# Stick-breaking attention summed by parts, with the value chain two tiles behind, 13 weight tiles and a woven last chunk

## The chip, the cores and the metric

The kernel runs on one NeuronCore of a Trainium2 chip. The metric is device time in microseconds (us) of one execution. TensorE (PE) does matrix products and transposes, VectorE (DVE), ScalarE (ACT) and GpSimd (POOL) do the elementwise work, SyncE (SP) issues nearly all DMAs, in order.

## What is computed

One decoder layer, 2048 tokens of 1024 numbers: a modulated RMS norm, one projection whose columns feed three token mixers (gated MLP, mLSTM, stick-breaking attention with 6 heads of 64), gates, an output projection and a residual. The change is in the attention:

```python
log_not = jnp.where(strict, jax.nn.log_sigmoid(-z), 0.0)
suffix = lax.cumsum(log_not, axis=3, reverse=True) - log_not
a = jnp.where(strict, jnp.exp(jax.nn.log_sigmoid(z) + suffix), 0.0)
outs.append(jnp.einsum('bhts,bshd->bthd', a.astype(vb.dtype), vb))
```

With b = sigmoid(z) and S[s] the product of (1 - b) over the keys from s on, a weight is a[s] = b[s] S[s+1], which is S[s+1] - S[s].

## The kernel before

Tokens are handled in 16 tiles of 128, in three blocks of 5, 5 and 6 tiles (`BLOCKS`). A block projects its tokens chunk by chunk of 384 columns (8 K-steps, three passes each because operands are split into a high and a low part, 24 matmuls for a token tile), and does the attention in three pairs of heads. For each pair `c_proj` makes q, k and v (evacuated by `c_evac` into Qst, Kst and Vst), then `stick` runs over units: one query tile i, one head h, up to four key tiles. A unit goes through `front` (two matmuls z, two sigmoids bb and be on ACT, masks on POOL, a running product backwards over bb on DVE, and the product be times bb, on DVE and POOL in turn), one step later `middle` (PE transposes, ACT copies the high part, DVE subtracts for the low part aT), another step later `back` (matmuls av with Vst), and `fin` (fold, copy yc, store). `interleave` mixes the units with the block's other projections, the fillers `bqk_proj`, `bg_proj`, `cz_proj`, `a_proj`; the value chunk of the mLSTM, `bv_proj` (tiles pv), follows the third pair. In the third pair of the first two blocks `get_x` also prepares the next block's x tiles, with a scaling on DVE and an addition on POOL (line 149). After the last block, pools are released and an output stage runs (out_proj, `mlstm`).

The order on each engine is set by a list scheduler that works with estimated times and priorities (`STK` puts stick ahead, `HIGH` the weight loads), so that instructions written later can stand earlier. Each engine then runs its own list strictly in order. The pools set further limits: `wr` holds 11 weight tiles, `bb` 4 and `be` 3 tiles of a unit.

Of the kernel before, what the change touches and what calls it, by code (L numbers as in the profile page):

```python
# [8 lines left out]
F32 = mybir.dt.float32  # L9
# [3 lines left out]
ALU = mybir.AluOpType  # L13
# [4 lines left out]
P = 128  # L18
# [14 lines left out]
def hybrid_block_kernel(ctx: ExitStack, tc: tile.TileContext, x, c, norm_g, w_ada, b_ada, w_in,  # L33
# [54 lines left out]

    lw = ExitStack()
    stg_p = lw.enter_context(tc.tile_pool(name="stg", bufs=2))  # L90
    wr_p = lw.enter_context(tc.tile_pool(name="wr", bufs=11))


    rs = ExitStack()
# [114 lines left out]
    brow = [stk.tile([P, 512], F32, tag="bb", bufs=4, name=f"brow{n}") for n in range(4)]  # L209
    for n in (2, 0, 3, 1):  # L210
        nc.gpsimd.memset(brow[n], 0.0)
    g_bc = [stk.tile([P, 512], F32, tag="be", bufs=3, name=f"g_bc{n}") for n in range(2)]

    def ada_load(half):
        for n, c0 in enumerate((1024 + 512 * half, 512 * half)):
# [86 lines left out]
    def c_proj(b, t0, nb, p):  # L302
# [17 lines left out]
            prev = nxt  # L320
        run(prev)

    def c_evac(b, t0, p, j, ps):
# [9 lines left out]
        nc.gpsimd.tensor_tensor(rr, rr, neghalf[:, 0:4], ALU.pow)  # L333
        nc.scalar.copy(Vst[:, i, :, 0:64], ps[:, 256:384].rearrange("p (h d) -> p h d", h=2))
        nc.vector.tensor_tensor(Vst[:, i, :, 64:128], ps[:, 256:384].rearrange("p (h d) -> p h d", h=2),
                                Vst[:, i, :, 0:64].bitcast(F32), ALU.subtract)
        qk = tmp.tile([P, 4, 2, 64], F32, tag="t512", bufs=T5, name=f"qk{p}_{i}")
        nc.vector.tensor_tensor(qk, ps[:, 0:256].rearrange("p (a d) -> p a d", a=4).unsqueeze(2)
                                .to_broadcast([P, 4, 2, 64]),
                                rr.unsqueeze(2).unsqueeze(3).to_broadcast([P, 4, 2, 64]), ALU.mult)  # L340
        yield
        pt = pat.tile([P, 4, P], F32, tag="at", name=f"pq{p}_{i}")
        for a in range(4):
            nc.tensor.transpose(pt[:, a, :], qk[:, a].rearrange("p r d -> p (r d)"), ident)
        ks = Kst[:, :, i * P:(i + 1) * P]
        gq, gk = prm[:, R_GQ:R_GQ + 1], prm[:, R_GK:R_GK + 1]
        nc.scalar.activation(ks, pt[:, 2:4, :], AF.Copy, scale=gk)
        nc.scalar.activation(Qst[:, j, 0], pt[:, 0:2, :], AF.Copy, scale=gq)
        nc.vector.scalar_tensor_tensor(ks[64:128], pt[64:128, 2:4, :], gk[64:128], ks[64:128].bitcast(F32),
                                       ALU.mult, ALU.subtract)  # L350
        nc.vector.scalar_tensor_tensor(Qst[:, j, 1], pt[:, 0:2, :], gq, Qst[:, j, 0].bitcast(F32),  # L351
                                       ALU.mult, ALU.subtract)
        if b < len(BLOCKS) - 1:
            nc.sync.dma_start(k_d[p][:, :, i * P:(i + 1) * P], ks.bitcast(F32))
            nc.sync.dma_start(v_d[p][:, i], Vst[:, i].bitcast(F32))

    def stick(p, t0, nb):
        units = []
# [450 lines left out]
    for b, nb in enumerate(BLOCKS):  # L809
# [22 lines left out]
        tail = bv_proj(t0, nb)  # L832
        if last:
            run(tail)
        else:
# [208 lines left out]
```

## Time and profile before

| | us |
|---|---|
| median of three runs (1478.18 to 1483.52) | 1481.43 |
| the profiled execution | 1480.27 |
| its span, first to last instruction | 1478.5 |
| PE busy | 1400.6 (95%) |
| DVE busy | 1025.1 (69%) |
| ACT busy | 678.1 (46%) |
| POOL busy | 647.3 (44%) |
| mean granted PE clock | 0.982 of full |

Busy time of PE is modelled at its ends and overlaps, so what counts for the end is where PE stands still (or runs at the lower clock), and which engine it waits for there. The stages of the span: setup until 76.6; the pairs of the first block from 76.6, 172.9 and 282.2; the second block's from about 377, 498.4 and 616.6; the last block's from 737, 909.7 and 1083.3; the output stage from 1215.6.

### The profile page before, as it was taken

The numbers are of one execution on the slowest core, as the hardware profiler recorded it, in microseconds if no ns is written. First come the engines' busy times: TensorE is split into PE (matmuls) and PEld (weight loads), VectorE is DVE, ScalarE is ACT, GpSimd is POOL, SyncE is SP. The second block draws the span as 40 slices with busy tenths as digits, with TensorE's granted clock in tenths as the row PEclk, the third lists the DMA queues.
The fourth block names the chain that finished last, engine by engine and source line by source line (L and its number), as shares of the span: only waits on it lengthen the run. The fifth ranks groups of instructions, "written<-read, shape, count | busy, mean of one in ns | idle before, by whom it ended". The sixth has DMA issues, their size and how long they took to land.

```text
span 1478.5 us, 24942 instructions
## 1 busy us (share of the span) xinstructions
PE 1400.6 (95%) x8468; PEld 1302.7 (88%) x8468; DVE 1025.1 (69%) x1778; ACT 678.1 (46%) x1656; POOL 647.3 (44%) x1140
## 2 busy tenths in 40 slices
PE   4999999889999999999999899999999978999998
PEld 3789999879999999988899799989999867888887
DVE  6796555586894566588698975778778888444443
ACT  3365444444464355446367655555455655211210
POOL 4463554573443433455233353433344336534442
PEclk9999999999999999999999999999999998999999
DMA  9866766657635534625332343303432524555551
GB/s 319 305 203 216 249 213 190 207 187 240 203 114 194 175 114 137 213 98 184 114 117 78 104 148 131 104 27 107 158 100 74 190 89 128 185 152 159 171 156 57
DMA packets 187103, 233.19 MB, mean 158 GB/s; under 512 B 22714, under 2 KB 160344, under 8 KB 186976
## 3 DMA queue, kind: packets, MB, share of 16 engines
q1 hardware_dynamic: 186752, 231.59, 48.1%
q8 instruction: 67, 1.10, 0.3%
q14 instruction: 60, 0.49, 0.1%
q0 software_dynamic: 224, 0.02, 0.0%
HBM read 159.24 MB, written 72.31 MB: 157 GB/s over the span
## 4 chain that ended last, share of the span: by engine, by line
PE 68%; DVE 16%; DMA 5%; issue 4%; POOL 3%; ACT 3%; SPq 1%; DVEq 0%; POOLq 0%; ACTq 0%
DVE bb L391 6%; PE av L421 5%; PE pc L296 4%; PE pc L298 4%; PE at L406 4%; PE pc L297 4%; PE po L957 4%; PE po L959 3%; PE po L958 3%; PE pg L298 3%; PE pg L297 3%; PE pg L296 3%; PE pb L465 2%; PE pb L464 2%; PE z L378 2%
## 5 line engine op out<-in xcount | busy, mean ns | idle before, releaser
L391 DVE TENSOR_TENSOR_SCAN bb<-bb,bb 128x513 f32<-128x513 f32 x144 | 194.1, 1348 | 24.9 <-ACT bb L383 23.8
L395 POOL TENSOR_TENSOR be<-be,bb 128x512 f32<-128x512 f32 (+3 forms) x120 | 133.0, 1108 | 148.3 <-DVE bb L391 69.2
L409 DVE TENSOR_TENSOR aT<-at,aT 128x512 fp32r<-128x512 f32 (+3 forms) x240 | 142.7, 597 | 31.5 <-ACT aT L408 30.5
L421 PE MATMUL av<-aT,Vst 128*128 128x256 f32 x816 | 146.4, 296 | 15.0 <-DVE aT L409 12.1
L408 ACT CAST aT<-at 128x512 fp32r<-128x512 f32 (+3 forms) x240 | 127.1, 530 | 70.3 <-PE at L406 67.4
L383 ACT ACTIVATE bb<-z 128x512 f32<-128x512 f32 (+3 forms) x240 | 130.3, 544 | 54.5 <-PE z L379 44.2
L421 PEld LDWEIGHTS av<-aT,Vst 128*128 128x128 f32 x816 | 120.5, 192 | 27.0 <-DVE aT L409 19.2
L296 PE MATMUL pc<-wr,hT 128*128 128x384 f32 (+1 forms) x384 | 136.8, 358 | 7.6 <-DVE hT L290 5.7
L406 PE MATMUL at<-ident,be 128*128 128x128 f32 x816 | 132.8, 277 | 9.6 <-DVE Qst L351 4.5
L298 PE MATMUL pc<-wr,hT 128*128 128x384 f32 (+1 forms) x384 | 135.5, 353 | 1.6 <-DVE hT L290 1.5
L297 PE MATMUL pc<-wr,hT 128*128 128x384 f32 (+1 forms) x384 | 134.0, 349 | 0.0
L384 ACT ACTIVATE be<-z 128x512 f32<-128x512 f32 (+3 forms) x240 | 132.1, 550 | 0.0
L406 PEld LDWEIGHTS at<-ident,be 128*128 128x128 f32 x816 | 99.2, 142 | 19.0 <-DVE aT L409 8.0
L957 PE MATMUL po<-wo,yT 128*128 128x512 f32 x256 | 105.0, 410 | 0.3 <-ACT yT L946 0.3
L958 PE MATMUL po<-wo,yT 128*128 128x512 f32 x256 | 102.3, 400 | 1.9 <-DVE wo L864 1.9
L391 DVE TENSOR_TENSOR_SCAN bb<-bb 128x129 f32<-128x129 f32 (+3 forms) x96 | 86.9, 905 | 23.5 <-POOL bb L386 16.3
L959 PE MATMUL po<-wo,yT 128*128 128x512 f32 x256 | 101.5, 400 | 0.0
L382 POOL MEMSET bb<- 128x1 f32 x240 | 24.2, 101 | 168.4 <-DVE bb L391 118.1
L378 PE MATMUL z<-Kst,Qst 128*128 128x512 f32 (+3 forms) x240 | 92.7, 387 | 1.7 <-ACT be L384 1.6
L466 PE MATMUL pb<-hT,wr 128*128 128x320 f32 (+1 forms) x288 | 91.9, 324 | 2.4 <-DVE wr L190 2.4
L464 PE MATMUL pb<-hT,wr 128*128 128x320 f32 (+1 forms) x288 | 93.1, 324 | 0.6 <-DMA wr<-w_d 0.6
L465 PE MATMUL pb<-hT,wr 128*128 128x320 f32 (+1 forms) x288 | 92.2, 322 | 0.0
(272 smaller groups left out, 3905.2 us busy)
## 6 DMA issues: line engine op xcount, KB each, us to landing
wr<-w_d SPq DMA_DIRECT2D x160, 384.0 KB, 5.6
w_d<-wr SPq DMA_DIRECT2D x80, 384.0 KB, 3.5
wad<-in_w_ada_dram SPq DMA_DIRECT2D x8, 1024.0 KB, 6.8
xo<-in_x_dram SPq DMA_DIRECT2D x16, 512.0 KB, 3.7
out_dram<-o SPq DMA_DIRECT2D x31, 256.0 KB, 2.9
xt<-in_x_dram SPq DMA_DIRECT2D x15, 512.0 KB, 3.5
st<-in_w_in_dram SPq DMA_DIRECT2D x60, 128.0 KB, 3.7
wr<-w_d SPq DMA_DIRECT2D x16, 392.0 KB, 6.0
```

The lines of the kernel that those rows point to most:

```text
L296: nc.tensor.matmul(ps, lhsT=hT[:, 0, k, cols], rhs=wt[k][:, 0, :W], start=k == 0, stop=False)
L297: nc.tensor.matmul(ps, lhsT=hT[:, 0, k, cols], rhs=wt[k][:, 1, :W], start=False, stop=False)
L298: nc.tensor.matmul(ps, lhsT=hT[:, 1, k, cols], rhs=wt[k][:, 0, :W], start=False, stop=k == KT - 1)
L384: nc.scalar.activation(be[:, :w], z[:, :w], AF.Sigmoid)
L391: nc.vector.tensor_tensor_scan(rev, rev, rev, carry.get((i, h), 1.0), ALU.mult, ALU.bypass)
L395: eng.tensor_tensor(be[:, :w], be[:, :w], bb[:, 1:w + 1], ALU.mult)
L406: nc.tensor.transpose(at[:, s, :], be[:, s * P:(s + 1) * P], ident)
L409: nc.vector.tensor_tensor(aT[:, :nb_, 1, :], at[:, :nb_, :], aT[:, :nb_, 0, :].bitcast(F32), ALU.subtract)
L421: nc.tensor.matmul(flat(av), lhsT=Vst[:, s0 + s, h, :], rhs=flat(aT[:, s]), start=(s0 + s == i), stop=(s0 + s == 0))
L957: nc.tensor.matmul(po, lhsT=yT[:, 0, k, :], rhs=wo[k][:, 0, cs], start=k == 0, stop=False)
L958: nc.tensor.matmul(po, lhsT=yT[:, 0, k, :], rhs=wo[k][:, 1, cs], start=False, stop=False)
L959: nc.tensor.matmul(po, lhsT=yT[:, 1, k, :], rhs=wo[k][:, 0, cs], start=False, stop=k == KT - 1)
```

## The change

The sum over keys is rearranged: with a[s] = S[s+1] - S[s], the sum of a[s] v[s] is the sum of S[s] (v[s-1] - v[s]) plus v of the query tile's last key. So a unit needs only the running product (bb): the second sigmoid, its mask, the column of ones and the product be times bb go, `middle` transposes bb, and bb gets 6 buffers. Vst now holds differences of values. They need each row's predecessor, one partition up: ACT copies v out of PSUM into vt, a DMA writes it one row lower into dv (127 rows), another fetches row 0, POOL subtracts vt, ACT copies the high part into Vst and POOL subtracts for the low part. That second half, `values`, is called two tiles later. The last value row goes to DRAM (vl_d), is read back to all partitions (vlast) and is added when yc is made, on DVE instead of ACT's copy. Weight tiles go from 11 to 13, the scratch of software DMAs is cut to 4096 bytes, and in the last block `bv_proj` becomes a filler of the third pair.

```diff
-    wr_p = lw.enter_context(tc.tile_pool(name="wr", bufs=11))
+    wr_p = lw.enter_context(tc.tile_pool(name="wr", bufs=13))
...
+    def values(pool_after, act_after):
+
+        b, p, i, dv, vt = late.pop(0)
+        with tc.issue_after(pool_after.ins):
+            nc.gpsimd.tensor_tensor(dv, dv, vt, ALU.subtract)
+        dv2 = dv.rearrange("p (h d) -> p h d", h=2)
+        with tc.issue_after(act_after.ins):
+            nc.scalar.copy(Vst[:, i, :, 0:64], dv2)
+        nc.gpsimd.tensor_tensor(Vst[:, i, :, 64:128], dv2, Vst[:, i, :, 0:64].bitcast(F32), ALU.subtract)
+        if b < len(BLOCKS) - 1:
+            nc.sync.dma_start(v_d[p][:, i], Vst[:, i].bitcast(F32))
+
     def c_evac(b, t0, p, j, ps):
...
-        nc.scalar.copy(Vst[:, i, :, 0:64], ps[:, 256:384].rearrange("p (h d) -> p h d", h=2))
-        nc.vector.tensor_tensor(Vst[:, i, :, 64:128], ps[:, 256:384].rearrange("p (h d) -> p h d", h=2),
-                                Vst[:, i, :, 0:64].bitcast(F32), ALU.subtract)
+        rr_pow = nc.gpsimd.tensor_tensor(rr, rr, neghalf[:, 0:4], ALU.pow)
...
+            nc.sync.dma_start(dv[0:1, :], v_before[p][P - 1:P, :])
...
+        v_copy = nc.scalar.copy(vt, ps[:, 256:384])
+        nc.sync.dma_start(dv[1:P, :], vt[0:P - 1, :])
+        nc.sync.dma_start(vl_d[p * NT + i:p * NT + i + 1, :], vt[P - 1:P, :])
+        v_before[p] = vt
+        late.append((b, p, i, dv, vt))
+        if j >= 2:
+            values(rr_pow, v_copy)
...
-            bb = stk.tile([P, 513], F32, tag="bb", bufs=4, name=f"bb{nm}")
-            be = stk.tile([P, 512], F32, tag="be", bufs=3, name=f"be{nm}")
-            nc.gpsimd.memset(bb[:, w:w + 1], 1.0)
-            nc.scalar.activation(bb[:, :w], z[:, :w], AF.Sigmoid, scale=-1.0)
-            nc.scalar.activation(be[:, :w], z[:, :w], AF.Sigmoid)
+            bb = stk.tile([P, 512], F32, tag="bb", bufs=BB, name=f"bb{nm}")
+            front_act[0] = nc.scalar.activation(bb[:, :w], z[:, :w], AF.Sigmoid, scale=-1.0)
...
-                nc.gpsimd.affine_select(out=be[:, w - P:w], in_=be[:, w - P:w], pattern=[[-1, P]],
-                                        compare_op=ALU.is_gt, fill=0.0, base=0, channel_multiplier=1)
...
+                    nc.sync.dma_start(vlast[i], vl_d[p * NT + i:p * NT + i + 1, :].broadcast_to([P, P]))
...
-            eng = nc.gpsimd if len(st_count) % 2 else nc.vector
-            st_count.append(0)
-            eng.tensor_tensor(be[:, :w], be[:, :w], bb[:, 1:w + 1], ALU.mult)
...
-            nc.scalar.copy(yc, py[:, 0:P])
+            nc.vector.tensor_tensor(yc, py[:, 0:P], vlast.pop(i), ALU.add)
...
+            if late and n >= 2:
+                values(front_pool[0], front_act[0])
...
+            fillers[2] = (chain(fillers[2][0], bv_proj(t0, nb)), 2)
```

What it moves: VectorE in the third pair of the last block, around the units of query tile 14. The names give the tile, query tile, head and first key tile. Before:

```order
L395 TENSOR_TENSOR be_14_1_4_14235<-be_14_1_4_14235,bb_14_1_4_14234 128x512
L391 SCALAR_TENSOR_TENSOR bb_14_1_0_14259<-bb_14_1_0_14259,bb_14_1_4_14234 128x513
L409 TENSOR_TENSOR aT_14_1_12_14220<-at_14_1_12_14216,aT_14_1_12_14220 128x3x128
L427 TENSOR_TENSOR avt_14_0_14229<-av_14_0_14122,avs_14_0_14227 128x128
L409 TENSOR_TENSOR aT_14_1_8_14249<-at_14_1_8_14244,aT_14_1_8_14249 128x4x128
L391 SCALAR_TENSOR_TENSOR bb_15_0_12_14287<-bb_15_0_12_14287 128x513
L395 TENSOR_TENSOR be_15_0_12_14288<-be_15_0_12_14288,bb_15_0_12_14287 128x512
```

The same place in the changed kernel:

```order
L418 SCALAR_TENSOR_TENSOR bb_14_1_0_13840<-bb_14_1_0_13840,bb_14_1_4_13816 128x512
L463 TENSOR_TENSOR yc_13_13724<-py_13_13721,vlast_13_13375 128x128
L433 TENSOR_TENSOR aT_14_0_4_13749<-at_14_0_4_13744,aT_14_0_4_13749 128x4x128
L418 SCALAR_TENSOR_TENSOR bb_15_0_12_13872<-bb_15_0_12_13872 128x512
L433 TENSOR_TENSOR aT_14_0_0_13776<-at_14_0_0_13771,aT_14_0_0_13776 128x4x128
L418 SCALAR_TENSOR_TENSOR bb_15_0_8_13901<-bb_15_0_8_13901,bb_15_0_12_13872 128x512
```

The products are gone, one addition for each query tile came, and running product and aT alternate, aT five units behind instead of three.

GpSimd at the passage from `c_proj` to `stick` in the same pair (rr: the norm of q and k of a token tile; bb of the tile 10: its masks). Before:

```order
L332 TENSOR_SCALAR rr_15_13199<-rr_15_13199 128x4
L333 TENSOR_TENSOR rr_15_13199<-rr_15_13199,neghalf 128x4
L386 AFFINE_SELECT bb_10_0_8_13228<-bb_10_0_8_13228 128x128
L388 AFFINE_SELECT be_10_0_8_13229<-be_10_0_8_13229 128x128
L395 TENSOR_TENSOR be_10_0_4_13265<-be_10_0_4_13265,bb_10_0_4_13264 128x512
```

Now:

```order
L351 TENSOR_TENSOR rr_15_12732<-rr_15_12732,neghalf 128x4
L333 TENSOR_TENSOR dv_13_12634<-dv_13_12634,vt_13_12636 128x128
L412 AFFINE_SELECT bb_10_0_8_12767<-bb_10_0_8_12767 128x128
L333 TENSOR_TENSOR dv_14_12685<-dv_14_12685,vt_14_12687 128x128
L337 TENSOR_TENSOR Vst<-dv_13_12634,Vst 128x2x64
L412 AFFINE_SELECT bb_10_1_8_12843<-bb_10_1_8_12843 128x128
```

The masks of the first units stand behind subtractions that wait for the shifted copies (dv).

TensorE where the last matmuls of `bv_proj` stand among the units of the third pair. Before:

```order
L297 MATMUL pv_14742<-wr_7_14595,hT 128x384
L298 MATMUL pv_14742<-wr_7_14595,hT 128x384
L421 MATMUL av_13_0_13885<-aT_13_0_12_13853,Vst 128x256 x2
L437 MATMUL py_12_13888<-fold,avt_12_1_13862 128x64
L378 MATMUL z_13_1_4_13995<-Kst,Qst 128x512
L379 MATMUL z_13_1_4_13995<-Kst,Qst 128x512
L406 MATMUL at_13_0_4_13907<-ident,be_13_0_4_13868 128x128 x4
```

Now:

```order
L300 MATMUL pv_14048<-wr_7_13530,hT 128x384
L583 MATMUL psp_10_0_13508<-va_10_12791,wsT 128x384
L301 MATMUL pv_14048<-wr_7_13530,hT 128x384
L407 MATMUL z_14_0_4_13697<-Kst,Qst 128x512
L408 MATMUL z_14_0_4_13697<-Kst,Qst 128x512
L445 MATMUL av_13_0_13459<-aT_13_0_4_13485,Vst 128x256
L583 MATMUL psp_10_1_13512<-va_10_12791,wsT 128x384
L445 MATMUL av_13_0_13459<-aT_13_0_4_13485,Vst 128x256 x3
L430 MATMUL at_13_0_0_13545<-ident,bb_13_0_0_13474 128x128 x4
```

The scheduler had already put pv among the units before; behind the last pv stood 18 z units and 22 units to transpose, and now 14 and 21.

## Rows read from the trace of the kernel before

**Rows 1.** Stages: window, length, busy of PE, PEld, DVE, ACT, POOL; clock; DMA

```profile
76.60:172.90 96.30, 93.04 (x599) 90.35 (x598) 68.78 (x130) 51.44 (x139) 50.85 (x96) 1.00 0.67 214
172.90:282.20 109.30, 104.79 (x614) 102.25 (x613) 61.41 (x125) 47.18 (x133) 51.54 (x90) 0.97 0.66 209
282.20:351.80 69.60, 63.94 (x387) 60.27 (x385) 50.80 (x96) 38.71 (x109) 46.12 (x81) 0.95 0.61 197
...
616.60:704.00 87.40, 80.97 (x507) 76.63 (x505) 74.34 (x116) 52.67 (x132) 53.02 (x93) 0.98 0.47 156
704.00:742.00 38.00, 35.11 (x208) 34.23 (x209) 23.55 (x47) 12.66 (x36) 9.65 (x17) 0.96 0.42 126
742.00:909.70 167.70, 161.88 (x1016) 153.12 (x1015) 137.46 (x226) 104.59 (x222) 66.88 (x136) 1.00 0.33 106
909.70:1083.30 173.60, 171.47 (x1085) 164.43 (x1084) 132.56 (x216) 90.06 (x214) 68.40 (x137) 1.00 0.34 112
...
1166.00:1215.60 49.60, 38.42 (x235) 30.79 (x234) 44.50 (x57) 31.26 (x67) 18.72 (x35) 0.93 0.49 179
1215.60:1251.00 35.40, 29.48 (x161) 25.69 (x159) 26.38 (x37) 17.79 (x42) 24.06 (x23) 0.81 0.46 130
```

**Rows 2.** What PE waited for: total us, times, longest

```profile
PE av L421 <- DVE aT L409: 12.1, 13, 3.0
...
PE at L406 <- DVE Qst L351: 4.5, 2, 3.2
...
PE pq L344 <- DVE qk L338: 3.8, 2, 3.4
...
PE pb L466 <- DVE wr L190: 2.4, 2, 1.3
```

**Rows 3.** Groups by line: count, busy us, mean ns, idle before

```profile
L395 POOL TENSOR_TENSOR be<-be,bb 128x512 f32<-128x512 f32 (+3 forms) x120 | 133.0, 1108 | 148.3 <-DVE bb L391 69.2 <-ACT be L384 21.1 <-PE at L406 17.0
...
L384 ACT ACTIVATE be<-z 128x512 f32<-128x512 f32 (+3 forms) x240 | 132.1, 550 | 0.0
...
L395 DVE TENSOR_TENSOR be<-be,bb 128x512 f32<-128x512 f32 (+3 forms) x120 | 77.4, 645 | 3.4 <-POOL be L388 0.4
...
L427 DVE TENSOR_TENSOR avt<-av,avs 128x128 f32<-128x128 f32 x96 | 26.8, 279 | 21.0 <-ACT avs L425 18.0 <-PE py L437 2.6
...
L544 POOL TENSOR_TENSOR gu<-tb 128x128 f32<-128x128 f32 x32 | 20.0, 626 | 29.5 <-DVE tb L543 28.6 <-PE at L406 0.8
```

**Rows 4.** Groups by line on DVE in 1166 to 1215.6 us

```profile
L391 DVE TENSOR_TENSOR_SCAN bb<-bb,bb 128x513 f32<-128x513 f32 x14 | 19.6, 1401 | 0.6 <-ACT bb L383 0.5
...
L395 DVE TENSOR_TENSOR be<-be,bb 128x512 f32<-128x512 f32 (+1 forms) x9 | 6.9, 763 | 0.2
```

**Rows 5.** Timeline of DVE and POOL, third pair: start, duration

```profile
1191.96 1.27 DVE L391 TENSOR_TENSOR_SCAN bb<-bb,bb 128x513 f32<-128x513 f32 x1
...
1193.73 1.84 DVE L391 TENSOR_TENSOR_SCAN bb<-bb,bb 128x513 f32<-128x513 f32 x1
...
1193.40 1.09 POOL L395 TENSOR_TENSOR be<-be,bb 128x512 f32<-128x512 f32 x1 [1.92 <-ACT bb L383]
```

**Rows 6.** Timeline of POOL and DVE at the second block's third pair

```profile
626.46 5.29 POOL L149 TENSOR_TENSOR xt<-xt,hshift 128x1024 f32<-128x1024 f32 x2
...
627.13 2.37 DVE L395 TENSOR_TENSOR be<-be,bb 128x256 f32<-128x256 f32 x1
629.42 3.40 DVE L391 TENSOR_TENSOR_SCAN bb<-bb,bb 128x513 f32<-128x513 f32 x1
```

**Rows 7.** Timeline of PE inside a projection: start, duration

```profile
257.92 0.34 PE L296 MATMUL pc<-wr,hT 128*128 128x384 f32 x1
258.09 0.34 PE L297 MATMUL pc<-wr,hT 128*128 128x384 f32 x1
```

**Rows 8.** Landing of the 64 KB stores of yc (line 440)

```profile
DMA to landing us min/median/max: 1.5/3.4/7.5
```

**Rows 9.** The page's DMA queue: packets, MB, share of 16 engines

```profile
q1 hardware_dynamic: 186752, 231.59, 48.1%
```

More of the change, by code (lines that the diff above doesn't have):

```diff
@@ L27 @@
 T5 = 6
+BB = 6
 OFF = dict(au=0, av=256, az=512, bq=768, bk=1152, bv=1536, bo=1920, bz=2304, bi=2688,
@@ L53, in hybrid_block_kernel @@
     v_d = [dram.tile([P, NT, 2, P], F32, name=f"v_d{p}") for p in range(3)]
+    vl_d = dram.tile([3 * NT, P], F32, name="vl_d")
     ident = const.tile([P, P], F32, name="ident")
@@ L75, in hybrid_block_kernel @@
     gates = const.tile([P, 2, NT, 4], F32, name="gates")
+    vt_end = const.tile([P, 3, P], F32, name="vt_end")
     gT = const.tile([P, 64], F32, name="gT")
@@ L208, in hybrid_block_kernel @@
     crow = tmp.tile([8, P], F32, tag="t512", bufs=T5, name="crow")
-    brow = [stk.tile([P, 512], F32, tag="bb", bufs=4, name=f"brow{n}") for n in range(4)]
+    brow = [stk.tile([P, 512], F32, tag="bb", bufs=BB, name=f"brow{n}") for n in range(4)]
     for n in (2, 0, 3, 1):
         nc.gpsimd.memset(brow[n], 0.0)
-    g_bc = [stk.tile([P, 512], F32, tag="be", bufs=3, name=f"g_bc{n}") for n in range(2)]
+    g_bc = [stk.tile([P, 512], F32, tag="bb", bufs=BB, name=f"g_bc{n}") for n in range(2)]
     def ada_load(half):
@@ L321, in c_proj @@
         run(prev)
+    late = []
+    v_before = {}
+    def values(pool_after, act_after):
[8 more added lines that the diff above has]
+            nc.sync.dma_start(v_d[p][:, i], Vst[:, i].bitcast(F32))
     def c_evac(b, t0, p, j, ps):
@@ L332, in c_evac @@
         nc.gpsimd.tensor_scalar(rr, rr, 1.0 / 64, EPS, ALU.mult, ALU.add)
-        nc.gpsimd.tensor_tensor(rr, rr, neghalf[:, 0:4], ALU.pow)
-        nc.scalar.copy(Vst[:, i, :, 0:64], ps[:, 256:384].rearrange("p (h d) -> p h d", h=2))
-        nc.vector.tensor_tensor(Vst[:, i, :, 64:128], ps[:, 256:384].rearrange("p (h d) -> p h d", h=2),
-                                Vst[:, i, :, 0:64].bitcast(F32), ALU.subtract)
+        rr_pow = nc.gpsimd.tensor_tensor(rr, rr, neghalf[:, 0:4], ALU.pow)
+        dv = tmp.tile([P, P], F32, tag="dv", bufs=4, name=f"dv{p}_{i}")
+        if i == 0:
+            nc.gpsimd.memset(dv[0:1, :], 0.0)
+        else:
+            nc.sync.dma_start(dv[0:1, :], v_before[p][P - 1:P, :])
+        vt = vt_end[:, p, :] if j == BLOCKS[b] - 1 else tmp.tile([P, P], F32, tag="vt", bufs=4, name=f"vt{p}_{i}")
+        v_copy = nc.scalar.copy(vt, ps[:, 256:384])
[5 more added lines that the diff above has]
+            values(rr_pow, v_copy)
         qk = tmp.tile([P, 4, 2, 64], F32, tag="t512", bufs=T5, name=f"qk{p}_{i}")
@@ L354, in c_evac @@
             nc.sync.dma_start(k_d[p][:, :, i * P:(i + 1) * P], ks.bitcast(F32))
-            nc.sync.dma_start(v_d[p][:, i], Vst[:, i].bitcast(F32))
     def stick(p, t0, nb):
@@ L369, in stick @@
         st = {}
-        st_count = []
+        vlast = {}
+        front_act, front_pool = [None], [None]
         def front(u):
@@ L379, in front @@
             nc.tensor.matmul(z[:, :w], lhsT=Qst[:, j, 1, h, :], rhs=kk, start=False, stop=True)
-            bb = stk.tile([P, 513], F32, tag="bb", bufs=4, name=f"bb{nm}")
-            be = stk.tile([P, 512], F32, tag="be", bufs=3, name=f"be{nm}")
-            nc.gpsimd.memset(bb[:, w:w + 1], 1.0)
-            nc.scalar.activation(bb[:, :w], z[:, :w], AF.Sigmoid, scale=-1.0)
-            nc.scalar.activation(be[:, :w], z[:, :w], AF.Sigmoid)
+            bb = stk.tile([P, 512], F32, tag="bb", bufs=BB, name=f"bb{nm}")
+            front_act[0] = nc.scalar.activation(bb[:, :w], z[:, :w], AF.Sigmoid, scale=-1.0)
             if s1 == i + 1:
-                nc.gpsimd.affine_select(out=bb[:, w - P:w], in_=bb[:, w - P:w], pattern=[[-1, P]],
+                front_pool[0] = nc.gpsimd.affine_select(out=bb[:, w - P:w], in_=bb[:, w - P:w], pattern=[[-1, P]],
                                         compare_op=ALU.is_gt, fill=1.0, base=0, channel_multiplier=1)
-                nc.gpsimd.affine_select(out=be[:, w - P:w], in_=be[:, w - P:w], pattern=[[-1, P]],
-                                        compare_op=ALU.is_gt, fill=0.0, base=0, channel_multiplier=1)
-            rev = bb[:, 0:w + 1][:, ::-1]
+                if h == 0:
+                    vlast[i] = stk.tile([P, P], F32, tag="vlast", name=f"vlast{p}_{i}")
+                    nc.sync.dma_start(vlast[i], vl_d[p * NT + i:p * NT + i + 1, :].broadcast_to([P, P]))
+            rev = bb[:, 0:w][:, ::-1]
             nc.vector.tensor_tensor_scan(rev, rev, rev, carry.get((i, h), 1.0), ALU.mult, ALU.bypass)
             carry[i, h] = bb[:, 0:1]
-            eng = nc.gpsimd if len(st_count) % 2 else nc.vector
-            st_count.append(0)
-            eng.tensor_tensor(be[:, :w], be[:, :w], bb[:, 1:w + 1], ALU.mult)
-            st[u] = [be, None]
+            st[u] = [bb, None]
             return 2 * w / 2.4
@@ L401, in middle @@
             nm = f"{p}_{i}_{h}_{s0}"
-            be = st[u][0]
+            bb = st[u][0]
             nb_ = s1 - s0
@@ L405, in middle @@
             for s in range(nb_):
-                nc.tensor.transpose(at[:, s, :], be[:, s * P:(s + 1) * P], ident)
+                nc.tensor.transpose(at[:, s, :], bb[:, s * P:(s + 1) * P], ident)
             aT = stk.tile([P, 4, 2, P], F32R, tag="aT", bufs=3, name=f"aT{nm}")
@@ L831, in hybrid_block_kernel @@
             interleave(stick(p, t0, nb), stick_cost(t0, nb), fillers[p][0], fillers[p][1] * chunk)
[L832 to L835, printed above, removed]
+        if not last:
+            tail = bv_proj(t0, nb)
             t1, n1 = t0 + nb, BLOCKS[b + 1]
@@ L1029 @@
     from concourse.bass_utils import run_bass_kernel_spmd as _run
[L1031 removed]
+    nc = _bacc.Bacc("TRN2", target_bir_lowering=False, num_devices=1, dynamic_dma_scratch_size=4096)
     arrays, args = {}, []
```

1 line of the change is left out of this document (removed).

## The prediction

> **What bounds the kernel now.** I read the busy shares first, then the table of stages, then the list of what PE waited for, and last the timelines of the stages with the largest gaps. PE is busy 95% of the span and none of its matmuls is taken away, so the gain can be no more than the time in which PE stands or runs at the lower clock. In each stage I take the window's length less PE's busy time as idle, and the length times (1 - granted clock) as the most that the clock costs; the clock has two levels, 1.2 and 2.4 GHz, and falls here after PE has stood still. From [rows 1] (idle / clock, us): 3.3 / 0 at 76.6; 4.5 / 3.3 at 172.9; 5.7 / 3.5 at 282.2; 6.4 / 1.7 at 616.6; 2.9 / 1.5 at 704; 5.8 / 0 at 742; 2.1 / 0 at 909.7; 11.2 / 3.5 at 1166. That is 41.9 + 13.5 = 55.4 us in the attention stages. The output stage's first 35 us hold another 5.9 / 6.7, before which no attention work stands. The largest waits of PE are for DVE: av for aT 12.1 us, transposes held by Qst 4.5, pq by qk 3.8 [rows 2]. In 1166 to 1215.6 DVE is busy 44.5 of 49.6 us and PE 38.4 [rows 1]: there the units are paced by DVE, since no filler is left.
>
> **The change part by part.**
>
> *Removed.* POOL loses 120 products, 133.0 us, ACT 240 sigmoids, 132.1 us, DVE 120 products, 77.4 us [rows 3]; with them go the masks of be and the memsets on POOL. DVE's subtraction for Vst moves to POOL. Nearly all of this stood beside PE work, so the sums are not the gain: each stage has its own.
>
> *Tail of the third pair, 1166 to 1215.6.* Here DVE sets the pace. Nine products, 6.9 us, go [rows 4]. The running products average 1401 ns over 14 [rows 4], and one alone takes 1.27 us, one beside a POOL product 1.84 [rows 5]; with those POOL products gone, 14 x (1.401 - 1.27) = 1.8 us more. Three additions for yc come in, each taken as long as the avt addition, 279 ns [rows 3]: 0.8 us back. The woven chunk changes little: the scheduler had already put pv among the units, and behind its last matmul stand 14 z units instead of 18, 21 to transpose instead of 22. That brings some running products under cover; I take 1.6 us, a little over one of them. Sum 6.9 + 1.8 - 0.8 + 1.6 = 9.5 us, of at most 11.2 + 3.5. At 49.6 - 9.5 = 40.1 DVE still has 35 us of work against PE's 38.4, so PE comes next.
>
> The row first: beside a POOL product of 1.09 us a running product grew by 0.57 us, and 14 of them by 1.8 us together [rows 4, 5]. The Trainium skill (SBUF — State Buffer, section Who interferes with whom) says that a DVE instruction with two SBUF inputs and a GpSimd one that reads SBUF exclude each other for the whole instruction. By that rule each of the seven or so products on POOL would cost DVE up to 1.09 us, some 7.6 us in place of 1.8, and the forecast would be 6 us lower; the measured 1.8 decides.
>
> *742 to 909.7.* Idle 5.8 us with DVE busy 137.5 of 167.7 [rows 1]; the waits are those of av and transposes for aT [rows 2]. A product less in every second unit on DVE frees 645 ns each [rows 3]. I take 4 us, between 0 (the wait is latency, not load) and 5.8.
>
> *Third pairs of the first two blocks, 282.2 and 616.6.* The two additions of get_x occupy POOL for 5.29 us, and next to them a DVE product of 256 columns took 2.37 us and a running product 3.40 [rows 6]; behind both stands the evacuation of Qst for which PE waited 3.2 us [rows 2]. get_x stays, but the product of 2.37 us goes. I take 4.5 us of 6.4 + 1.7 at 616.6, and 4.5 of 5.7 + 3.5 at 282.2, where the same step stands; bounds 0 and all of it.
>
> *172.9 to 282.2.* PE waited 3.4 us for qk once [rows 2], and the clock fell. vt frees the PSUM tile sooner and two more weight tiles are fetched ahead, but whether the cause goes isn't seen: I take 2.5 of 7.8 us.
>
> *76.6 to 172.9.* The waits for weights being split, 2.4 us [rows 2], are what two more weight tiles and a freer POOL would shorten: 2 of 3.3 us. *704 and 909.7*: 1 and 1.5 us of 4.4 and 2.1.
>
> *The value chain* is what is added, for each of 48 token tiles: two POOL subtractions, 96 x 626 ns = 60 us [rows 3], less than half of what POOL loses; one more ACT copy, paid by the yc copy that ACT loses; and four DMAs (SP's list grows by 197 rows). I cost it at nothing because of its place: the shifted copy is issued when vt is there and wanted two tiles later, two times 24 matmuls at 0.17 to 0.18 us apart [rows 7], 8.4 us. A store of the same 64 KB lands after 3.4 us in the median and 7.5 at most [rows 8]. If that cover is gone, what waits is POOL's subtraction, and behind it in the same queue the norm of the next token tile (then qk, pq) and the masks of the first units (then the running product); ACT's copy into Vst also stands ahead of Kst and Qst evacuations. In the first two blocks the store of Vst follows it on SP, among weight loads. The price then is the first rival's.
>
> *The handover at 1215.6* keeps its steps: 0, between 12.6 us gained and 6 lost if the loads for the output stage, which wait for pv's weight buffers, come later than they did.
>
> **Sum.** 9.5 + 4 + 4.5 + 4.5 + 2.5 + 2 + 1 + 1.5 = 29.5 us. The profiled execution took 1480.3, 1.2 under the median of 1481.4; as a median the forecast is 1481.4 - 29.5 = 1452 us.
>
> **The rivals.**
>
> *The shifted value rows come too late (slower).* One partition up means 127 rows. Should this copy not be spread like the others but run on one DMA engine, the queue's rows give its time: 0.481 x 16 x 1478.5 us over 186752 packets is 61 ns each, over 231.59 MB it is 20 bytes in a ns [rows 9]; 127 packets of 512 bytes are 3.2 us by bytes, 7.7 by packets. With 1.5 us, the shortest landing [rows 8], that is 4.7 to 9.2 us against the 8.4 of cover, and the longest landings lie 4 us above the median. If every second of 48 tiles comes 1.5 us late, POOL and PE lose 36 us and the time is 1452 + 36 = 1488. From 0.6 us a tile on (29.5 / 48) it eats the whole gain. For it: the copy has no twin in the trace before. Against it: 3.2 us by bytes is nearer, since packets here average 1240 bytes. Chance 9%. The Trainium skill (DMA: Bandwidth & Descriptors, section Why a DMA increments its semaphore by 16 and not by 1) says that a transfer's engines must divide its slowest dimension, so that 127 partitions go to one engine; no row before can show that, and the rival's price does not need it.
>
> *Only the tail and the loaded stage gain.* The waits before 742 come with get_x's additions, with weight splitting and DMAs, which all stay; then 9.5 + 4 = 13.5 us, 1468. For it: POOL's additions alone slowed a running product to 3.40 us [rows 6]. Against it: the product between them goes. 20%.
>
> *Every wait of the attention stages goes*: 55.4 us, 1426. For it: ACT and POOL are each some 130 us lighter, and aT runs five units behind, not three. Against it: the tail can't lose its drain, and some waits have other causes. 13%.
>
> *PE bounds it all the same*: waits move to other places, first to the handover, which runs at a clock of 0.81 [rows 1], and the time stays at 1481. 8%.
>
> **How the numbers follow.** The forecast's case has 50%, its own range 1440 to 1464 from half and all of its uncertain terms. A measurement of this kernel can tell about 0.3%, 4.4 us, from no change. Faster: 50 + 20 + 13 = 83%; the same 8%; slower 9%. The range from 1432 to 1480 leaves out the late copies, half of the case in which every wait goes, and a little of the last.
>
> **What would show it.** Right: in the tail running products near 1.27 us and DVE no longer ahead of PE in busy time, the last pair some 9 us shorter, the third pairs of the first two blocks 4 to 5 each, no wait of POOL for the shifted copies. Wrong: pq or the first running product of a pair waiting for POOL behind dv; the copies of 127 rows landing past 8 us; the stretch from the last av to the first long run of output matmuls longer than before; or gaps of the get_x stages as they were.

## The result and the profile after

The changed kernel takes 1514.53 us (median, 1514.11 to 1520.51) against 1481.91 for the kernel before: ratio 1.0238, 95% interval 1.0216 to 1.0259. It is slower by 2.4%; the forecast was 1452, with a range to 1480. The profiled execution spans 1512.4 us, 33.9 more than before.

The page of the changed kernel: span, busy time, share and instructions of each engine, and its DMA queue, which answers to [rows 9].

```profile
span 1512.4 us, 24156 instructions
...
PE 1410.5 (93%) x8468; PEld 1312.5 (87%) x8468; DVE 939.8 (62%) x1658; ACT 577.5 (38%) x1416; POOL 503.5 (33%) x783
...
q1 hardware_dynamic: 201344, 237.91, 49.0%
```

DVE, ACT and POOL lost 85, 101 and 144 us of work, as the change intends, and PE waits longer all the same: of the 33.9 us, PE stands 24.0 longer and is busy 9.9 longer, at a mean granted clock of 0.974 for 0.982. Where, the windows tell (columns as in [rows 1], after's own stages).

```profile
82.50:183.50 101.00, 95.36 (x602) 90.91 (x602) 66.22 (x126) 49.26 (x130) 45.49 (x79) 1.00 0.70 226
183.50:294.20 110.70, 103.63 (x610) 101.19 (x609) 53.61 (x116) 42.36 (x120) 42.25 (x70) 0.97 0.67 208
294.20:363.80 69.60, 56.97 (x317) 54.15 (x316) 42.24 (x83) 28.04 (x84) 37.01 (x55) 0.88 0.56 180
...
398.40:532.60 134.20, 123.85 (x785) 118.57 (x784) 87.85 (x158) 53.63 (x130) 35.38 (x72) 0.96 0.50 163
...
1199.20:1248.80 49.60, 40.84 (x263) 34.33 (x262) 36.94 (x51) 22.05 (x46) 5.06 (x6) 0.97 0.61 202
```

Idle time (length less PE) is 12.6 us in the 69.6 from 294.2, where [rows 1] had 5.7, and the clock is 0.88 for 0.95. It is 10.4 us at 398.4, a stage that had next to none (PE 120.4 of 121.1 us before). The losses are in setup and the first two blocks. Setup and the first block load, split and store weights (the last weight store is issued at 337.1 us); the second block reads them back, as the third does. A row for each stage, from the first z of a pair to that of the next, in us, difference to before; the last three columns are runs told of below:

| stage of before | before | forecast | changed | no copies | split copy | by DRAM |
|---|---|---|---|---|---|---|
| 0 to 76.6 (setup) | 76.6 | 0 | +5.9 | +0.7 | +2.5 | +4.7 |
| 76.6 | 96.3 | -2 | +4.7 | -2.2 | +1.1 | +0.4 |
| 172.9 | 109.2 | -2.5 | +1.5 | -7.4 | -6.3 | -8.5 |
| 282.2 | 95.1 | -4.5 | +9.1 | +2.4 | +3.0 | +7.1 |
| 377.3 | 121.1 | 0 | +13.1 | +1.4 | +5.8 | +2.1 |
| 498.4 | 118.3 | 0 | +2.3 | -0.4 | -0.7 | -0.5 |
| 616.6 | 120.3 | -5.5 | +2.3 | -7.3 | -3.1 | -8.2 |
| 736.9 | 172.8 | -4 | -1.4 | -5.4 | -5.0 | -5.6 |
| 909.8 | 173.6 | -1.5 | -3.3 | -5.9 | -6.5 | -5.7 |
| 1083.3 (to the last py) | 131.8 | -9.5 | -0.5 | -3.9 | -4.0 | -2.6 |
| output | 263.4 | 0 | +0.2 | +0.6 | +0.3 | -0.1 |

What the engines waited for in the changed kernel (waiter and line, what ended it: total us, times, longest):

```profile
ACT wr L192 <- DMA st<-in_w_in_dram: 79.4, 27, 9.6
...
ACT Vst L336 <- POOL dv L333: 64.9, 25, 8.3
...
POOL dv L333 <- DMA dv<-vt_end: 35.9, 7, 7.9
...
PE z L407 <- ACT bb L410: 15.8, 10, 5.3
...
POOL dv L333 <- DMA dv<-vt: 13.1, 7, 5.9
```

Before, the first of these was:

```profile
ACT wr L189 <- DMA st<-in_w_in_dram: 50.9, 22, 7.2
```

and PE's z waited little for ScalarE:

```profile
PE z L378 <- ACT be L384: 1.6, 5, 0.6
```

GpSimd does wait for the shifted rows (49 us), as the first rival said, and 35.9 of it is for the last token tile of a block (vt_end). In the second and the last block the transfers of those copies make five of the fifteen longest pieces of the chain of work that ended last (start, length):

```profile
542.37 7.11 DMA dv<-vt_end
...
666.24 6.50 DMA dv<-vt_end
...
781.34 8.40 DMA dv<-vt_end
...
952.44 8.73 DMA dv<-vt_end
...
1123.18 7.82 DMA dv<-vt_end
```

But the largest new wait of PE, z held by bb, has another chain behind it, in the first block. SyncE's list at the second pair of the first block (start, time of the issue):

```profile
185.77 0.65 SPq L360 DMA_DIRECT2D dv<-vt  x1
186.48 1.00 SPq L361 DMA_DIRECT2D vl_d<-vt  x1
187.53 0.55 SPq L357 DMA_DIRECT2D dv<-vt  x1
188.17 1.23 SPq L196 DMA_DIRECT2D w_d<-wr  x2
189.45 0.76 SPq L171 DMA_DIRECT2D st<-in_w_in_dram  x1
...
193.72 0.68 SPq L360 DMA_DIRECT2D dv<-vt_end  x1
194.45 2.37 SPq L361 DMA_DIRECT2D vl_d<-vt_end  x1
```

and what waits, ScalarE's weight copy and then PE (in brackets idle time and what ended it):

```profile
194.12 0.93 ACT L192 CAST wr<-st 128x384 fp32r<-128x384 f32 x2 [9.57 <-DMA st<-in_w_in_dram]
...
196.31 0.69 PE L407 MATMUL z<-Kst,Qst 128*128 128x384 f32 x1 [4.41 <-ACT bb L410]
```

SyncE issues here without a pause, the weight piece (st) goes out at 189.45, ScalarE stands at its split until 194.12, and the Qst copy and the sigmoids behind it are late for PE. The row store (L361, one row of 512 bytes) mostly takes long to issue where it follows the shifted copy at once (columns: min/median/max ns, first and last start):

```profile
L361 SPq DMA_DIRECT2D vl_d<-vt x39: 294/999/4812, 62.1 to 1122.0; - x39
L361 SPq DMA_DIRECT2D vl_d<-vt_end x9: 1461/2370/4204, 88.3 to 1123.9; - x9
```

48 of them are 74.9 us of SyncE's time, for a DMA that moves 24 KB in all.

### The profile page after: what moved, and what is told of

Same layout as the page of the kernel before. It is cut to its first block, busy times and chain, and to the rows that moved or that the text cites. A ratio compares the mean times of both kernels' runs of the same rounds, so it can differ in the third digit from the quotient of the medians.

```text
span 1512.4 us, 24156 instructions
## 1 busy us (share of the span) xinstructions
PE 1410.5 (93%) x8468; PEld 1312.5 (87%) x8468; DVE 939.8 (62%) x1658; ACT 577.5 (38%) x1416; POOL 503.5 (33%) x783
## 4 chain that ended last, share of the span: by engine, by line
PE 62%; DMA 12%; DVE 11%; issue 4%; ACT 4%; POOL 3%; SPq 3%; DVEq 0%; POOLq 0%; ACTq 0%
PE av L445 5%; PE at L430 4%; PE po L982 4%; PE po L984 4%; PE po L983 4%; PE pc L299 4%; DVE bb L418 4%; PE pc L301 4%; PE pc L300 4%; DMA st<-in_w_in_dram 3%; DMA dv<-vt_end 3%; DMA wr<-w_d 2%; PE z L407 2%; PE z L408 2%; PE pg L301 2%
## 5 line engine op out<-in xcount | busy, mean ns | idle before, releaser
L418 DVE TENSOR_TENSOR_SCAN bb<-bb,bb 128x512 f32<-128x512 f32 x144 | 190.1, 1320 | 15.1 <-ACT bb L410 13.6
L445 PE MATMUL av<-aT,Vst 128*128 128x256 f32 x816 | 145.6, 293 | 17.9 <-DVE aT L433 11.2
L430 PE MATMUL at<-ident,bb 128*128 128x128 f32 x816 | 133.0, 278 | 7.2 <-DVE Qst L380 3.2
L430 PEld LDWEIGHTS at<-ident,bb 128*128 128x128 f32 x816 | 101.0, 143 | 15.1 <-DVE aT L433 4.8
L412 POOL TENSOR_SCALAR_AFFINE_SELECT bb<-bb 128x128 f32<-128x128 f32 x96 | 40.4, 422 | 180.5 <-ACT bb L410 148.4
L418 DVE TENSOR_TENSOR_SCAN bb<-bb 128x128 f32<-128x128 f32 (+3 forms) x96 | 83.3, 869 | 25.8 <-POOL bb L412 25.2
L490 PE MATMUL pb<-hT,wr 128*128 128x320 f32 (+1 forms) x288 | 95.4, 331 | 4.0 <-ACT wr L192 3.1
L299 PE MATMUL pa<-wr,hT 128*128 128x384 f32 x256 | 90.6, 354 | 6.7 <-DMA wr<-w_d 4.0
L491 PE MATMUL pb<-hT,wr 128*128 128x320 f32 (+1 forms) x288 | 94.2, 328 | 0.0
L492 PE MATMUL pb<-hT,wr 128*128 128x320 f32 (+1 forms) x288 | 93.7, 328 | 0.0
L299 PE MATMUL pg<-wr,hT 128*128 128x384 f32 x256 | 89.5, 350 | 1.8 <-DMA wr<-w_d 1.8
```

Of the source, the lines that this page charges most:

```text
L299: nc.tensor.matmul(ps, lhsT=hT[:, 0, k, cols], rhs=wt[k][:, 0, :W], start=k == 0, stop=False)
L430: nc.tensor.transpose(at[:, s, :], bb[:, s * P:(s + 1) * P], ident)
L445: nc.tensor.matmul(flat(av), lhsT=Vst[:, s0 + s, h, :], rhs=flat(aT[:, s]), start=(s0 + s == i), stop=(s0 + s == 0))
```

## The experiments

Theory A: the copy of 127 rows as a transfer does the harm, through SyncE's list (later split into A1, the list held, and A2, the one DMA engine). Theory B: its rows are late for GpSimd. Theory C: the order, the weave or the 13 tiles. Medians stand against 1479 to 1482 for the kernel before, run beside them.

**Parts of the value chain taken out.**

```
e1:  - store of the row vl_d, - read of vlast      (yc adds ident)
e2:  - dma_start(dv[1:P], vt[0:P-1])               dv = vt - vt
e3:  - all four DMAs                               dv = vt - vt, yc adds ident
e4:  - dma_start(dv[1:P, :], vt[0:P-1, :])
     + dma_start(dv[1:113, :], vt[0:112, :])
     + dma_start(dv[113:P, :], vt[112:P-1, :])
```

> The changed kernel without the 48 stores of the last value row and the 48 broadcast reads of it (yc adds a constant tile in their place, so the last value row is missing from the output); the shifted copies stay. Theory A (SyncE's list: in the first two blocks SP issues DMAs back to back, the row stores alone take 74.9 us of issue and the reads 22.3, and weight loads stand behind them): most of the 33 us comes back, 1480 to 1492. Theory B (the shifted copies land late, GpSimd waits 49 us for them and all else follows): little changes, 1505 to 1515. Theory C (13 weight tiles, the weave and the new order of the weight splits are to blame): 1508 or more.

> The changed kernel without the copies of 127 rows (GpSimd subtracts the tile from itself, so the value differences are zero); the one-row copies, the row stores and the reads stay. Theory A: 31.8 us of issue go, and if the row stores' issue is long only because they follow a copy that runs on one DMA engine, their median falls from 1.19 us to 0.5 and another 45 us go: 1485 to 1495; if their issue stays long, 1500 or more. Theory B: GpSimd no longer waits for dv, 1465 to 1480. Theory C: 1508 or more.

> The changed kernel without all four DMAs of the value chain (shifted copy, one-row copy, row store, broadcast read; value differences zero, last row missing). The arithmetic on GpSimd and ScalarE stays. Theories A and B both: the forecast of the rest was right but for the tail, 1455 to 1472. Theory C: 1490 or more.

> The changed kernel, complete, with the copy of 127 rows written as 112 and 15 rows, two DMAs. If the 127 rows run on one DMA engine (packets 25 ns apart, 3.2 us) and 112 do not, the copy lands some 2.5 us sooner and the row store's issue is short. Theory A: 48 more issues of 0.6 us are added, about 45 us of long row stores go, 1500 to 1512. Theory B: GpSimd's 49 us of waits shrink by half or more, 1485 to 1500. Theory C: no change, 1510 to 1518.

Measured: e1 1499.19 (ratio 1.0117, 1.0096 to 1.0137); e2 1460.57 (0.9867, 0.9850 to 0.9885); e3 1453.50 (0.9820, 0.9804 to 0.9835); e4 1467.53 (0.9911, 0.9896 to 0.9927). C falls with e3. The complete kernel with the copy merely cut in two is 47 us faster than the changed one, and faster than before, although it issues 48 DMAs more. No theory had that much (A gave e4 1500 at best, B 1485). Two more lie outside every range: e1 between A and B, and e2 below both. e3 is 1.5 us under its range. The copy also leaves its mark in the landing records (the updates of a DMA's semaphore in the trace): one of 127 rows leaves two, one of 112 rows sixteen. In e2 the row stores are short:

```profile
L360 SPq DMA_DIRECT2D vl_d<-vt x39: 215/271/627, 61.3 to 1062.4; - x39
L360 SPq DMA_DIRECT2D vl_d<-vt_end x9: 241/382/437, 78.7 to 1068.1; - x9
```

In e1, which has none, the next DMA behind the copy, the one-row copy L357, takes their place, with a median of 1.0 us and up to 4.8.

**Is it the wait or the transfer?** e5 copies into a spare tile dx that nobody reads; e6 gives the rows a tile more of time, but those of a block's last tiles, behind which no tile follows, only a unit more; e7 replaces the copy by a way of two full ones.

```
e5:  - dma_start(dv[1:P], vt[0:P-1])     + dma_start(dx[1:P], vt[0:P-1])     dv = vt - vt
e6:  - if j >= 2: values(...)            + if j >= 3: values(...)            dv, vt: 5 buffers
e7:  - row copy, shifted copy, row store
     + dma_start(vs_d[p][P + i*P : P + (i+1)*P], vt)
     + dma_start(dv, vs_d[p][P + i*P - 1 : P + (i+1)*P - 1])     vlast read from vs_d
```

> The changed kernel with the copy of 127 rows kept, but into a spare tile that nothing reads (GpSimd subtracts the tile from itself, so the value differences are zero). The transfer and its issue stay, the wait of GpSimd and ScalarE for its rows goes. Theory A (the copy on one DMA engine holds SyncE's next issue and that engine, so weight loads come late): 1495 to 1512, row stores still above 1 us of issue. Theory B (the rows come late to GpSimd and ScalarE): near the run without the copy (1460.6), 1460 to 1472.

> The changed kernel, complete, with the second half of the value chain called three token tiles later instead of two (dv and vt get five buffers). Theory A: the copies are as many and as slow, 1506 to 1520. Theory B: another 4.2 us of cover for each copy, GpSimd's 49 us of waits for dv nearly go, 1470 to 1490.

> The changed kernel, complete, with the value rows stored to DRAM (128 rows), and dv read from there one row lower (128 rows, the one-row copy is contained in it); the last row for yc is read from the same place, so the separate row store goes: three DMAs a token tile instead of five in the run with the split copy, none of 127 rows. Theory A: issue shrinks by some 40 us against the split copy (1467.5), 1455 to 1465. Theory B: the read must wait for the store, so rows land 2 to 3 us later than there, 1467 to 1485.

Measured: e5 1499.30 (1.0126, 1.0107 to 1.0145); e6 1507.09 (1.0181, 1.0156 to 1.0206); e7 1461.52 (0.9873, 0.9844 to 0.9902). Of the 54.0 us between the changed kernel and e2, the copy that nobody awaits keeps 38.7; the waits for its rows are the other 15.2, and e6 gets back 7.4 us (GpSimd still waits 31.0 us for dv there). By stages e5 loses 33.0 us in setup and the first two blocks, where the changed kernel loses 38.9, and gains 16.2 in the last, where the changed kernel gains 5.2. So the transfer costs in setup and the first two blocks, and its late rows cost mostly in the last block (11 us).

But e5 does not free GpSimd altogether. dv still gets its first row by the one-row copy (L357), which stands in SyncE's list behind the long one, and GpSimd waits 24.8 us for it, six times, at the last tile of a pair. At the first pair of the second block the row store's issue (L362) is held for 3.94 us, the one-row copy goes out behind it, and GpSimd waits, with the masks of bb behind it in its list:

```profile
408.71 3.94 SPq L362 DMA_DIRECT2D vl_d<-vt  x1
...
413.81 0.61 SPq L357 DMA_DIRECT2D dv<-vt  x1
```

```profile
417.08 0.40 POOL L333 TENSOR_TENSOR dv<-vt_end 128x128 f32<-128x128 f32 x1 [5.61 <-DMA dv<-vt]
417.43 0.29 POOL L413 TENSOR_SCALAR_AFFINE_SELECT bb<-bb 128x128 f32<-128x128 f32 x1
```

Against e2, e5 loses 21.2 us in setup and the first block and 18.0 in the second. What part of the 18.0 comes by this wait no run separates. So theory B, as the wait for the copy's own rows, is a part; the larger part is what the copy does to the issues behind it, weight pieces in the first block and other rows too.

**List or engine?** e8 issues the spare copy from ScalarE's queue. e10 and e11 leave the 127 rows out and hold SyncE with one-row copies instead, e11 at the head of the list. e12 is e5 with 112 rows.

```
e8:  e5 with  nc.scalar.dma_start(dx[1:P], vt[0:P-1])
e10: e2 with  for r in range(5): dma_start(dx[r:r+1], vt[r:r+1])
e11: e2 with  with prio(-4000): for r in range(4): dma_start(dx[r:r+1], vt[r:r+1])
e12: e5 with  dma_start(dx[1:113], vt[0:112])
```

> The run with the unawaited copy of 127 rows (1499.3 against 1460.6 without the copy), with that copy issued from ScalarE's DMA queue instead of SyncE's; its rows are again read by nobody and the value differences are zero. Theory A1 (what hurts is that SyncE's next issue is held behind the copy): SyncE is no longer held, ScalarE pays 48 issues of about 0.7 us, 1462 to 1475. Theory A2 (what hurts is the one DMA engine, which all transfers that use it wait for, whoever issues the copy): 1490 to 1502, and SyncE's issues still lengthened.

> The run without the copy of 127 rows (1460.6, value differences zero), with five small copies in its place for each token tile, one row each, from SBUF to a spare tile that nothing reads. One such copy takes about 0.57 us of SyncE's issue, so SyncE is held for about as long as by the unawaited copy of 127 rows (in the first two blocks 412 us of issue with it, 329 without, 2.7 us a token tile), but no DMA engine gets more than five packets of 32 bytes from them. Theory A1 (SyncE's list held: what stands behind is issued late): 1485 to 1503, near the run with the unawaited copy (1499.3). Theory A2 (the one DMA engine that holds 127 packets): 1461 to 1470.

> The run without the copy of 127 rows (1460.6, value differences zero) with four small copies to a spare tile, one row each, at the head of SyncE's list as soon as a token tile's v is there: SyncE is held for some 2.3 us at each, ahead of the weight loads and stores of the projection. Theory A1 (the hold at this place): 1485 to 1503. Theory A2 (the engine that holds 127 packets): 1465 to 1478, as the same issues behind the weight loads gave (1474).

> The run with the unawaited copy (1499.3), the copy cut from 127 to 112 rows: as many DMAs, nearly the same lists, but 16 engines instead of one. Both theories: the row store's issue falls below 0.6 us in the median and the time to 1461 to 1470. Should it stay above 1485, the number of DMAs and not the engine is to blame.

Measured: e8 1493.71 (1.0084, 1.0055 to 1.0113); e10 1474.05 (0.9946, 0.9929 to 0.9964); e11 1465.08 (0.9896, 0.9862 to 0.9930); e12 1463.63 (0.9882, 0.9859 to 0.9905). e10 lies between the ranges of A1 and A2. In e8 the time fits A2 but its sign does not: the row stores are short again. SyncE now waits for the copies themselves, 64 us in all:

```profile
SPq L417 <- DMA dx<-vt: 14.0, 4, 5.9
...
SPq L186 <- DMA dx<-vt: 11.0, 4, 5.6
```

e8 is no clean test, for ScalarE pays too: 30 us for the 48 issues, and 11.0 us of waiting for the copies before Kst. But it shows what the held list hides. The weight pieces issued within 5 us behind a copy landed after 6.3 us in the median (10 pieces), the others after 3.8.

More issue by itself costs little: until the last block starts e10 adds 110 us of it (439 against 329 in e2; e5 has 412) and 13.5 us of time in all, e11 192 copies of 0.6 us and 4.5. So a list that is merely fuller is not the cause. e12 differs from e5 in 15 rows and is 35.7 us faster; both theories asked for that, and what it rules out is the number of DMAs. What is left has parts of A1 and A2: a transfer that is not spread, and that holds what comes behind it. The same stretch of SyncE's list shows how it gets at the weights. e5:

```profile
172.86 0.64 SPq L357 DMA_DIRECT2D dv<-vt  x1
173.60 0.68 SPq L361 DMA_DIRECT2D dx<-vt  x1
174.38 2.03 SPq L196 DMA_DIRECT2D w_d<-wr  x1
...
178.34 1.53 SPq L417 DMA_DIRECT2D vlast<-vl_d  x1
...
188.02 0.71 SPq L171 DMA_DIRECT2D st<-in_w_in_dram  x1
...
192.69 0.93 ACT L192 CAST wr<-st 128x384 fp32r<-128x384 f32 x2 [9.34 <-DMA st<-in_w_in_dram]
```

and e12:

```profile
167.22 0.56 SPq L357 DMA_DIRECT2D dv<-vt  x1
167.88 0.55 SPq L361 DMA_DIRECT2D dx<-vt  x1
168.53 0.58 SPq L196 DMA_DIRECT2D w_d<-wr  x1
...
170.92 0.61 SPq L417 DMA_DIRECT2D vlast<-vl_d  x1
...
178.46 0.62 SPq L171 DMA_DIRECT2D st<-in_w_in_dram  x1
...
182.98 0.93 ACT L192 CAST wr<-st 128x384 fp32r<-128x384 f32 x2 [3.75 <-DMA st<-in_w_in_dram]
```

The same 18 issues from the first line to the weight piece take 15.2 us in e5 and 11.2 in e12. What is issued behind the copy is held, a weight store here (2.03 for 0.58), a read of vlast there (1.53 for 0.61). The piece itself needs as long from issue to ScalarE, 4.7 and 4.5 us, and all 96 pieces land after 3.9 us in the median in both runs. It is late because it is issued late; PE then waited 4.17 us for bb in e5, and not at all at that place in e12. That e10 and e11 hold the list too and lose less I put down to the scheduler, which knew of their issues and set weight loads ahead of them, while it can't know of the hold; no run tested that, so this last link is open.

**Weight tiles, weave, fewer reads.** Each is a change to a faster kernel of the above; e9 and e13 read vlast for several tiles at once.

```
e4_wr11:     e4 with  tile_pool(name="wr", bufs=11)
e7_noweave:  e7 without  fillers[2] = (chain(fillers[2][0], bv_proj(t0, nb)), 2)
e9:          e7 with one vlast read for a pair, at the start of stick
e13:         e7 with two: tiles 0 and 1 at the start, the rest at the third tile's first unit
```

> The run with the split copy (1467.5) with 11 weight tiles instead of 13. If two more tiles were worth what the forecast put on the weight waits (2 us at 76.6 and a part of the 2.5 at 172.9): 1469 to 1473. If they are worth nothing: 1465 to 1469.

> The run that goes by DRAM (1461.5) with the last block's eighth chunk again after the third pair and not woven into it. If the weave is worth the 1.6 us that the forecast gave it: 1462 to 1466. If the order of the scheduler puts the chunk in the same place anyway: 1459 to 1464. If the weave is what shortens the third pair: 1466 to 1472.

> The run that goes by DRAM (1461.5) with the last value rows of all token tiles of a block read by one DMA for each pair instead of one for each token tile: 9 reads instead of 48, some 17 us less of SyncE's issue, nothing left out. Theory A: 1455 to 1460. If SyncE's list no longer decides, or this read holds the list until the last tile's store has landed: 1460 to 1466.

> The run that goes by DRAM (1461.5), complete, with the last value rows read by two DMAs a pair (tiles 0 and 1; the rest once the third tile's first unit is due) instead of one a tile: 18 reads instead of 48 and none that stands in SyncE's list before its rows have landed. If the loss of the run with one read (1487.8) was its wait in the list: 1456 to 1464. If merging the reads itself does harm (rows in fewer, larger transfers, another order): 1475 or more.

Measured: e4_wr11 1468.95 (0.9921, 0.9901 to 0.9941) and e7_noweave 1460.41 (0.9869, 0.9835 to 0.9903), neither to be told from its parent; e9 1487.80 (1.0046, 1.0029 to 1.0062); e13 1463.45 (0.9876, 0.9850 to 0.9902). e9 saved 39 issues and lost 26 us, far outside both expectations. Its read stands in SyncE's list until the last tile's store has landed, with reads of dv behind it:

```profile
SPq L397 <- DMA vs_d<-vt_end: 17.8, 5, 5.4
```

```profile
POOL dv L336 <- DMA dv<-vs_d: 48.6, 13, 7.6
```

In e7 that second wait was 18.2 us. e13, whose reads come when their rows are there, loses nothing, and gains nothing either: the number of issues no longer decides. The best complete versions, e7 and e7_noweave, are 1.3% faster than the kernel before.

## Why the prediction was wrong, step by step

**The value chain, costed at nothing: the step that failed.** I gave it 0 us on the ground that the copy "is issued when vt is there and wanted two tiles later", with 8.4 us of cover, and named as its only price the waits behind late rows. With all four DMAs left out the kernel takes 1453.5 us, where I forecast 1452; with them 1514.5. Leaving out the copy alone gives back 54.0 of these 61 us. (POOL's 96 subtractions took 48.8 us, under the 60 I counted.) Both halves of the ground failed. By the trace of after the copy is issued 3.2 us after vt is written in the median and 12.3 at most, since SyncE, in order, comes to it late; its rows land 9.1 us after vt in the median, past 8.4 in 26 of 48 tiles. And the last tile of a block is not followed by two more: there they land after 14.8 us in the median, and there GpSimd waits most (35.9 of 49.0 us).

**The first rival** had the place and the sign, but a price of 36 us by a path that carries 15 for the copy's own rows (e5; more with the one-row copies held behind it), and only 9% of the chance. I bounded the landing by 4.7 and 9.2 us and let the byte rate decide. From issue to landing the trace of after gives 6.2 us in the median and 9.0 at most (from the landing records; 3.0 in the median for the 112 rows of e4), so the bound held, but only from the issue on. What I left out is that a slow transfer is not private: it delays what is issued behind it. Row stores landed 5.4 us after their issue in the median, and 2.3 without the copy. I had even counted that SyncE's list grows by 197 rows (the trace has 1012 DMA issues for 823), and gave no price to the list.

The Trainium skill (DMA: Bandwidth & Descriptors, section Why a DMA increments its semaphore by 16 and not by 1) says that a transfer uses the largest number of engines up to 16 that divides the slowest dimension, one for 127 partitions. The runs agree: 127 rows to 112 is 1499.3 to 1463.6 us, landing 6.2 to 3.1, landing records two to sixteen. I had cited the rule and weighed it below a byte rate from transfers that were spread; a rule that the change hits exactly deserved more than that.

**The tail.** Forecast -9.5, measured -0.5, and -3.9 without the copies. The products went, as counted. The running product did get cheaper, as these rows of after show for [rows 4] (the last 49.6 us of the pair):

```profile
L418 DVE TENSOR_TENSOR_SCAN bb<-bb,bb 128x512 f32<-128x512 f32 x13 | 17.1, 1318 | 0.0
L433 DVE TENSOR_TENSOR aT<-at,aT 128x512 fp32r<-128x512 f32 (+2 forms) x22 | 14.4, 653 | 8.0 <-ACT aT L432 7.9
...
L463 DVE TENSOR_TENSOR yc<-py,vlast 128x128 f32<-128x128 f32 x3 | 0.8, 278 | 1.5 <-PE py L461 1.5
```

13 x (1401 - 1318) is 1.1 us, between my 1.8 and nothing. I had set the 1.8 against 7.6 us, my estimate by the rule of mutual exclusion of the Trainium skill (SBUF — State Buffer, section Who interferes with whom). My estimate was off, not the rule: I charged every product on POOL to DVE, and the trace of before agrees with an exclusion that holds up whichever starts second. In the window of [rows 4] three running products of 513 columns, each begun some 0.33 us after a product on POOL, took 1.83 to 1.85 us. One that had begun 0.38 us before such a product took 1.28, and the product on POOL took 1.79 instead of 1.09:

```profile
1183.93 1.79 POOL L395 TENSOR_TENSOR be<-be,bb 128x512 f32<-128x512 f32 x1 [0.35 <-ACT be L384]
```

The yc addition cost 278 ns, as taken. But DVE is busy 36.9 of 49.6 us and PE 40.8, and neither paces: DVE now waits 7.9 us for ScalarE's aT copies. I read this as a chain of latencies that took over from load, which my step "so PE comes next" did not allow for; no run tests it. The weave, put at a gain of 1.6, gave none that can be seen: the third pair takes 129.2 us in e7 and 125.8 without it, but the output stage is then 1.3 us longer, and the whole kernel takes 1461.5 and 1460.4, which can't be told apart.

**Near in sum, by other shares.** That 1453.5 without copies comes so near to 1452 is in good part luck, for the terms miss in both directions. Without copies the last block's first two pairs gain 5.4 and 5.9 us (forecast 4 and 1.5), 172.9 gains 7.4 (2.5), 616.6 gains 7.3 (5.5), and 282.2 loses 2.4 (forecast -4.5). The handover at 0 was right (+0.6 over the whole output stage). Two more weight tiles are worth 1.4 us in the medians, within what can't be told from nothing.

**Wrong signs to look for.** I had named as proof of the contrary rows that land past 8 us and a wait of the unit chain behind dv. Both are there, but the other large wait, ScalarE for weight pieces, was not on the list.

## What to carry to other kernels

Do not shift by one partition with a DMA of 127 rows: here it cost 47 us more than 112 and 15 rows in two DMAs, and 53 more than a store and a read of 128 rows by DRAM. Price a new transfer not only by who waits for its data but by what is issued behind it: where a queue issues without a pause, a hold of one or two microseconds reaches the loads that stand after it. Count a transfer's cover from where its issue stands in the list, not from when its data is there, and look at the last tile apart. And a read that must wait for its data belongs in an in-order list no earlier than where the data is there; merging reads to save issues cost 26 us when that was broken.

## What the runs showed of the hardware that was not expected

- The issue of a 512-byte row store took 1.0 us in the median (2.4 for the last tile of a block) and up to 4.8 directly behind the copy of 127 rows, 0.27 without it and 0.44 behind a copy of 112 rows.
- With the slow copy on ScalarE's queue SyncE's issues were short again, and yet e8 kept 33 of e5's 39 us: SyncE waited 64 us for the copies, ScalarE paid 30 us for their issue, and weight pieces issued just behind a copy landed after 6.3 us instead of 3.8.
- Cutting the copy into two transfers, with 48 issues more, made the changed kernel 3.1% faster.
